# The MLP of a streaming encoder layer: up projection by Strassen's block product, down projection from DRAM, output projection by token halves

## The chip, the cores and the metric

The kernel runs on one core of a Trainium2 chip. The metric is the device time of one execution in microseconds; a kernel's time is the median of its runs. The profile comes from one execution. Its engines are TensorE (PE in the profile, with PEld for its weight loads), VectorE (DVE), ScalarE (ACT), GpSimd (POOL) and SyncE (SP, which here only issues DMAs).

## The reference

One layer of a streaming encoder for two groups, 1024 prompt tokens and 64 sample tokens, all in float32 with a width of 1024:

```python
x = x + mix @ p["w_out"][li]
x = x + cross_attention(rms_norm(x, p["norm_x_g"][li]), mem_k[li], mem_v[li],
                        p["xq_w"][li], p["xo_w"][li])
h = rms_norm(x, p["norm_ffn_g"][li])
x = x + jnp.square(jax.nn.relu(h @ p["w_up"][li])) @ p["w_down"][li]
...
return rms_norm(x, p["final_g"]), ...
```

`mix` comes from three token mixers (a gated recurrence, a convolution, a pooling mixer), which the change doesn't touch. `w_up` is 1024 x 4096, `w_down` 4096 x 1024, and the attention's output weight `xo_w` 1024 x 1024. `rms_norm` multiplies by the reciprocal root of the mean square of a token and by a gain for each channel.

## The kernel before

**Layout.** Activations lie with the channels on the 128 partitions and the 1088 tokens (T) in a row: eight tiles of 128 channels (KT = 8), each in a slot of 1152 floats. The slots are one pool of 35; a tile takes a slot and gives it back after its last reader.

**Products.** Each float32 operand is split in two parts that one pass of TensorE carries: `hi` is a copy on ACT into the type `fp32r`, `lo` the difference on DVE. `mm3` (L186) makes a product from three matmuls: hi by hi, hi by lo, lo by hi. `dense` (L195) makes one output tile of 128 channels: for each of the three token groups of 364, 364 and 360 columns it takes a PSUM bank, adds up 8 x 3 matmuls, and calls an evacuation. With `across` it runs the groups side by side. PSUM has four banks of the tag "d" and four of "m".

**Weights.** `fetch` (L136) loads the next block of 128 x 8 x 128 weights through SP, into one of three buffers; `prep` (L155) makes its hi part on ACT and its lo part on DVE, into one of three buffers each, and fetches the next. `weights` (L168) takes the oldest prepared block. The order of the blocks is `all_weights` (L966).

**Output projection.** `residual` (L741) loads a residual tile, makes one dense output tile, adds the two in the evacuation on DVE, squares the sum on ACT and adds it up on DVE for the norm (`sq_add`), splits it times the gain (`hl`), and stores the tile to DRAM. The norm's root enters later: `rstd_rows` makes one factor for each token, broadcast over the partitions (`rb`).

**MLP.** `mlp` (L886) goes through 8 blocks of 512 hidden channels. For each it makes 4 dense tiles of the up projection; the evacuation multiplies the relu by `rb`, and `squared` squares and splits the result. Then it makes 8 dense tiles of the down projection over these 4 and adds each to the residual in SBUF (`xr`, loaded from DRAM in the first block). The last block goes by other token groups and ends in the final norm and the stores.

**Order.** The scheduler puts each engine's instructions in an order when the program is built, and each engine then runs its own strictly in that order, waiting where a semaphore says so. SP, too, issues its DMAs in order: a DMA that waits holds those behind it.

Of the kernel before, what the change touches and what calls it, by code (L numbers as in the profile page):

```python
# [11 lines left out]
P = 128  # L12
D = 1024
# [22 lines left out]
TT = [(c * P, min(P, T - c * P)) for c in range(9)]  # L36

# [10 lines left out]
class Trunk:  # L48
# [87 lines left out]
    def fetch(self, parts=1):  # L136
        s = next(self.wsrc, None)
# [6 lines left out]
        self.raws.append(raw)  # L144
# [10 lines left out]
    def prep(self, parts=1):  # L155
        if not self.raws:
            return
        raw = self.raws.pop(0)
# [14 lines left out]
    def pump(self):  # L173
        """traces the next steps of each chain that runs beside the dense products"""
# [11 lines left out]
    def mm3(self, out, wh, wl, xh, xl, first, last):  # L186
        mm = self.mm
        mm(out, wh, xh, start=first, stop=False)
        mm(out, wh, xl, start=False, stop=False)
        mm(out, wl, xh, start=False, stop=last)  # L190
# [56 lines left out]
    def sq_add(self, acc, x):  # L247
        """adds x*x to the running sum of squares"""
        if acc is None:
            acc = self.slot(n="acc")  # L250
            self.act(acc[:, :T], x, AF.Square)
            return acc
        sq = self.slot(n="sq")
        self.act(sq[:, :T], x, AF.Square)
        self.tt(acc[:, :T], acc[:, :T], sq[:, :T], ADD)
        return acc

    def hl(self, full, g):
        """parts of full * g that one pass carries exactly"""
# [112 lines left out]
    def sq_two(self, accs, k):  # L372
        """sums of squares in two halves, joined before the last"""
# [41 lines left out]
    def mixers(self, xs):  # L415
# [11 lines left out]
        # convolution inputs  # L427
# [60 lines left out]
    def head(self, h, f, k, q, vT, ons):  # L488
# [18 lines left out]
        # v, token-major  # L507
# [56 lines left out]
        # k, token-major  # L564
# [11 lines left out]
        # states  # L576
# [19 lines left out]
        # outputs, token-major for the norm, then transposed  # L596
# [27 lines left out]
    def conv(self, glus, mix):  # L624
# [12 lines left out]
        # layer norm over the channels, token-major  # L637
# [116 lines left out]
    def attention(self, acc, hs):  # L754
# [19 lines left out]
        # a unit: 4 prompt tiles of one head, or the sample tiles of two heads  # L774
# [20 lines left out]
        return [self.outs[k] for k in range(KT)]  # L795
# [60 lines left out]
    def att_values(self, unit, ph, pl):  # L856
# [5 lines left out]
        for h, s, c, n in jobs:  # L862
            kh, kl = self.kv[g, h]
            for dv in range(2):
                if 2 * h + dv not in self.outs:
                    self.outs[2 * h + dv] = (self.slot(F32R, n="oh"), self.slot(F32R, n="ol"))
                oh, ol = (x[:, s:s + n] for x in self.outs[2 * h + dv])
# [4 lines left out]
                self.act(oh, ps[:, :n], AF.Copy)  # L872
                self.split_lo(ol, ps[:, :n], oh)

# [11 lines left out]
    def mlp(self, acc, hs, x2src):  # L886
        nc = self.nc
        rb = self.rstd_rows([acc], D)
        xr = []
        facc = None  # L890
        for fb in range(NFB):
            ts = []
            for f in range(FB):
                t = self.slot(n="t")

                def ev(b, t0, m):
                    self.stt(t[:, t0:t0 + m], b, 0.0, rb[:, t0:t0 + m], MAX, MUL)
                self.dense(self.weights(), hs, range(KT), ev, across=f == 0 and fb == 0)
                ts.append(self.squared(t, GROUPS if f == FB - 1 else [(0, T)]))
            if fb == 0:  # L900
                for o in range(KT):
                    x = self.slot(n="xr")
                    nc.sync.dma_start(x[:, :T], x2src[o])
# [219 lines left out]
```

## Time and profile before

| | |
|---|---|
| runs, us | 1605.22, 1608.7, 1605.95 (median 1605.95) |
| span of the profiled execution, us | 1606.3 |
| busy, us | PE 1575.2, DVE 781.2, ACT 476.6, POOL 92.0 |
| matmuls | 9732 |
| moved by DMA | 107.47 MB, 67 GB/s over the span |
| square sums of attention's output projection (`acc`), first to last start, us | 738.6 to 823.8 |
| first evacuation of a down product (into `xr`), us | 879.1 |

The profiled execution is known by its span, 1606.3 us; it lies 0.4 us over the median of the runs. A row of a group names line, engine, operation, tiles as out<-in, partitions x elements, and the count; then the busy us in all and the mean ns of one; then the engine's idle us before them, and what ended it. The duration of a matmul covers its whole way through the array, and matmuls overlap: what one costs is the distance from start to start. In a timeline a row begins with its start and its length in us.

### The profile page before, as it was taken

To read this page: it belongs to the slowest core of one execution; us is meant where nothing else is said; L and a number is where in the kernel's file an instruction comes from. 1 tells how busy PE (TensorE), PEld (TensorE's weight loads), DVE (VectorE), ACT (ScalarE), POOL (GpSimd) and SP (SyncE) were. 2 spreads that over 40 slices of the span, in tenths; PEclk is the share of its full clock that TensorE was granted. 3 is DMA by queue.
4 is the path that set the end of the run, shared out by engine and by line. 5 is a ranking of instruction groups with operands and counts; after the bars stand their busy time and mean duration, and the time that the engine had idled before them with its cause. 6 is when DMAs were issued, how large, how long until landed. Compare 5 with 4: busy or idle time off the path is not lost.

```text
span 1606.3 us, 22499 instructions
## 1 busy us (share of the span) xinstructions
PE 1575.2 (98%) x9732; PEld 1542.7 (96%) x9732; DVE 781.2 (49%) x1123; ACT 476.6 (30%) x807; POOL 92.0 (6%) x59
## 2 busy tenths in 40 slices
PE   7899998999999999999999999999999999999997
PEld 7699998899999999989999999999999999999997
DVE  7838868865654433683433333333332433333344
ACT  7611142436262222462232121120301212021144
POOL 2720004100000000000000000000000000000005
PEclk9899999999999999999999999999999999999999
DMA  8421010101013311212424111111111111111103
GB/s 311 144 83 41 28 31 16 41 14 43 29 64 143 123 54 53 79 67 83 152 94 151 40 53 40 40 53 40 41 52 40 45 47 40 53 40 40 53 1 112
DMA packets 37555, 107.47 MB, mean 67 GB/s; under 512 B 5456, under 2 KB 13136, under 8 KB 37456
## 3 DMA queue, kind: packets, MB, share of 16 engines
q1 hardware_dynamic: 34576, 105.38, 19.7%
q8 instruction: 76, 1.25, 0.3%
q10 hardware_dynamic: 2880, 0.66, 0.2%
q14 instruction: 23, 0.19, 0.0%
HBM read 89.94 MB, written 16.08 MB: 66 GB/s over the span
## 4 chain that ended last, share of the span: by engine, by line
PE 85%; issue 9%; DVE 3%; POOL 1%; ACT 1%; DMA 0%; SPq 0%; POOLq 0%; DVEq 0%; ACTq 0%
PE psd L193 75%; PE psm L193 4%; PE psm L530 3%; DVE cacc L130 1%; POOL xr L126 1%; DVE wl L127 1%; PE psm L608 0%; PE psm L610 0%; PE psm L501 0%; PE psd L850 0%; DMA wr<-wk 0%; ACT wh L119 0%; PE psm L619 0%; PE psm L582 0%; PE psm L547 0%
## 5 line engine op out<-in xcount | busy, mean ns | idle before, releaser
L193 PE MATMUL psd<-hi,wl 128*128 128x364 f32 (+3 forms) x2400 | 793.6, 331 | 3.0 <-DVE wl L127 3.0
L193 PE MATMUL psd<-lo,wh 128*128 128x364 f32 (+3 forms) x2400 | 792.9, 330 | 3.3 <-DVE lo L130 3.3
L193 PE MATMUL psd<-hi,wh 128*128 128x364 f32 (+3 forms) x2400 | 793.2, 331 | 0.0
L193 PEld LDWEIGHTS psd<-lo,wh 128*128 128x128 f32 x2400 | 453.1, 189 | 5.0 <-DVE lo L130 4.6
L193 PEld LDWEIGHTS psd<-hi,wl 128*128 128x128 f32 x2400 | 453.6, 189 | 3.6 <-DVE wl L127 3.2
L193 PEld LDWEIGHTS psd<-hi,wh 128*128 128x128 f32 x2400 | 453.7, 189 | 1.2
L119 ACT ACTIVATE wh<-wr 128x1024 fp32r<-128x1024 f32 (+1 forms) x127 | 131.8, 1039 | 815.6 <-PE psd L193 655.5
L127 DVE TENSOR_TENSOR xr<-psd,xr 128x364 f32<-128x364 f32 (+3 forms) x192 | 101.9, 534 | 210.2 <-PE psd L193 210.0
L127 DVE TENSOR_TENSOR wl<-wr,wh 128x1024 fp32r<-128x1024 f32 (+1 forms) x127 | 167.2, 1320 | 66.8 <-ACT wh L119 66.8
L130 DVE SCALAR_TENSOR_TENSOR t<-psd,rb 128x364 f32<-128x364 f32 (+1 forms) x96 | 51.1, 533 | 202.4 <-PE psd L193 202.4
L130 DVE SCALAR_TENSOR_TENSOR cacc<-glu,vecs,cacc 128x1118 f32<-128x1118 f32 x60 | 90.5, 1508 | 0.7
L126 POOL TENSOR_TENSOR xr<-xr,facc 128x416 f32<-128x416 f32 x16 | 19.0, 1224 | 1193.7 <-ACT facc L119 1193.7
L127 DVE TENSOR_TENSOR res<-psd,res 128x364 f32<-128x364 f32 (+1 forms) x45 | 23.2, 533 | 92.2 <-PE psd L193 51.2
L127 DVE TENSOR_TENSOR lo<-t,hi 128x1088 fp32r<-128x1088 f32 (+2 forms) x48 | 43.8, 913 | 39.9 <-ACT hi L119 39.9
L193 PE MATMUL psd<-ol,wh 128*128 128x364 f32 (+1 forms) x168 | 55.2, 329 | 0.0
L193 PE MATMUL psd<-oh,wl 128*128 128x364 f32 (+1 forms) x168 | 55.2, 329 | 0.0
L193 PE MATMUL psd<-oh,wh 128*128 128x364 f32 (+1 forms) x168 | 55.2, 328 | 0.0
L530 PEld LDWEIGHTS psm<-q,fn 128*128 128x128 f32 (+2 forms) x448 | 48.0, 180 | 4.5 <-issue 3.9
L530 PE MATMUL psm<-q,fn 128*128 128x64 f32 (+2 forms) x448 | 49.0, 262 | 2.4 <-DVE tot L127 2.4
L119 ACT ACTIVATE t<-t 128x1088 f32<-128x1088 f32 (+2 forms) x48 | 38.3, 799 | 35.1 <-DVE t L130 35.1
L130 DVE SCALAR_TENSOR_TENSOR qf<-psd,rb 128x364 f32<-128x364 f32 (+1 forms) x24 | 12.7, 535 | 57.1 <-PE psd L193 57.1
L119 ACT ACTIVATE hi<-t 128x1088 fp32r<-128x1088 f32 (+2 forms) x48 | 38.9, 810 | 1.5
(214 smaller groups left out, 1442.7 us busy)
## 6 DMA issues: line engine op xcount, KB each, us to landing
wr<-w_up SPq DMA_DIRECT2D x32, 512.0 KB, 3.6
wr<-w_down SPq DMA_DIRECT2D x32, 512.0 KB, 3.5
wr<-w_in SPq DMA_DIRECT2D x22, 512.0 KB, 3.5
x<-res SPq DMA_DIRECT2D x16, 544.0 KB, 2.7
x<-xT SPq DMA_DIRECT2D x8, 544.0 KB, 7.3
res<-xT SPq DMA_DIRECT2D x8, 544.0 KB, 5.1
res<-x SPq DMA_DIRECT2D x8, 544.0 KB, 4.9
xr<-x SPq DMA_DIRECT2D x8, 544.0 KB, 7.6
```

Of the source, the lines that this page charges most:

```text
L119: return self.inorder("act", lambda: self.nc.scalar.activation(out, in_, f, **kw))
L126: return self.inorder("pool", lambda: eng.tensor_tensor(out, a, b, op))
L127: return self.inorder("dve", lambda: self.nc.vector.tensor_tensor(out, a, b, op))
L130: return self.inorder("dve", lambda: self.nc.vector.scalar_tensor_tensor(out, in0, s, in1, op0, op1))
L193: return self.inorder("pe", lambda: self.nc.tensor.matmul(*args, **kw))
L530: mm(pv[:m, c], k[:, c * P:c * P + m], qc[:, :, 1, :], start=True, stop=True)
```

## The change

The change has three parts.

1. **Output projection by halves.** The 1088 tokens are two halves of 544 (H), each of two quarters of 272 (Q). `project` makes the output projection for one half, in groups of 272 columns, with two output tiles in one slot; the weights `xo` are therefore fetched and prepared twice. `attention` writes its results into tiles by half, so the unit of tokens 512 to 1023 is evacuated in pieces of 32 and 480 columns.
2. **Up projection by Strassen's product** (Winograd's form). `normed_half` now multiplies the norm into the activations. `operands` takes the 2 x 2 blocks of a half (channels 0 to 511 and 512 to 1023 by quarter) and makes the seven right operands from them: four differences (two on DVE, two on POOL), then hi on ACT and lo on DVE of all seven, 14 slots for a half. `pair_units` takes the weights of a pair of output tiles as 2 x 2 blocks, makes four sums on POOL and splits seven left operands in four units "12", "56", "73" and "4". `up` runs seven products of 12 matmuls with 272 columns for each pair and half, in the order 1, 5, 6, 2, 7, 3, 4. Several products add up in one bank (A: 1, 6, 7, 4; C: 5, 3; B: 2), and the partial sums are evacuated in between, on ACT or DVE. The last steps form relu(v) times v on DVE, and each half of a pair is stored to DRAM (`tdram`, "tt" in the rows). The first two pairs run for half 0 alone at the start and for half 1 alone at the end; 14 pairs run for both.
3. **Down projection as a stage of its own.** `mlp` calls `up`, then loads the residual and, block by block, the four tiles of t, splits them and makes the down products as before. Block 0 goes last.

```diff
+H = T // 2
+Q = H // 2
+NPAIR = 16
+LATE = 2
+FBS = list(range(1, NFB)) + [0]
...
+    def project(self, c, os, src, spill):
...
+            self.dense(self.weights(), os, range(KT), ev, groups=[(0, Q), (Q, Q)])
+            acc = self.sq_add(acc, x, H)
+            if o % 2:
+                nc.sync.dma_start(spill[o - 1:o + 1, :, cols].rearrange("o p t -> p o t"), xs[-1])
...
+    def normed_half(self, acc, xs, g):
+        r = self.rstd_cols([acc], CT, D, "m")
...
+        for k in range(KT):
+            x = xs[k // 2][:, k % 2]
+            self.stt(x, x, self.vec(g, k), rb[:, :H], MUL, MUL)
...
+    def operands(self, xs):
...
+        b11, b12, b21, b22 = block(0, 0), block(0, 1), block(1, 0), block(1, 1)
+        r = {}
+        r["1"] = split(b11)
+        t1, w1 = diff(b12, b11)
+        r["5"] = split(t1, w1)
+        t3, w3 = diff(b22, b12, gp)
+        t2, w2 = diff(b22, t1)
+        r["6"] = split(t2, w2)
+        r["2"] = split(b21)
+        t4, w4 = diff(b21, t2, gp)
+        r["7"] = split(t3, w3)
+        r["3"] = split(b22)
+        r["4"] = split(t4, w4)
...
+    def pair_units(self):
...
+        self.tt(s12[:, :4], rj[:, :4], rj[:, 4:], ADD, gp)
+        self.tt(s12[:, 4:], s12[:, :4], ri[:, :4], SUB, gp)
+        self.tt(s34[:, :4], ri[:, :4], rj[:, :4], SUB, gp)
+        self.tt(s34[:, 4:], ri[:, 4:], s12[:, 4:], SUB, gp)
...
+        for src, k0, names in ((ri, 0, "12"), (s12, 0, "56"), (s34, 0, "73"), (rj, 4, "4")):
...
+            self.act(hi[:, :n], src[:, k0:k0 + n], AF.Copy)
+            self.split_lo(lo[:, :n], src[:, k0:k0 + n], hi[:, :n])
...
+    ORDER = "1562734"
+    BANK = {"1": "A", "5": "C", "6": "A", "2": "B", "7": "A", "3": "C", "4": "A"}
...
+    def up(self, xs, tdram):
+        jobs = [(p, (0,)) for p in range(LATE)] + [(p, (0, 1)) for p in range(LATE, NPAIR)]
+        jobs += [(p, (1,)) for p in range(LATE)]
...
+            for i, m in enumerate(self.ORDER):
+                for c in cs:
...
+                    for k in range(4):
+                        self.mm3(banks[b][:, :Q], wh[:, k], wl[:, k], th[:, k], tl[:, k], k == 0 and m in "152", k == 3,
...
+                    if m in "1564":
+                        self.act({"1": c11, "5": c22, "6": c12, "4": c21}[m], ps, AF.Copy)
+                    else:
+                        d = {"2": c11, "7": c22, "3": c12}[m]
+                        self.tt(d, ps, d, ADD)
+                    if m in "34":
+                        v = t[:, "34".index(m)]
+                        self.stt(v, v, 0.0, v, MAX, MUL)
...
+            for c in cs:
+                self.nc.sync.dma_start(tdram[2 * p:2 * p + 2, :, c * H:c * H + H].rearrange("o p t -> p o t"), st[c][1])
...
+        nxt = block(FBS[0])
+        for i, fb in enumerate(FBS):
+            ts = nxt
+            if i < NFB - 1:
+                nxt = block(FBS[i + 1])
...
+        for c in range(2):
+            acc, xs = self.project(c, o[c], x1, x2)
...
+            if c == 0:
+                halves[0] = operands()
+        self.mlp(halves, x2)
```

**What moves, at three places.** The first is DVE in the output projection. Before, each tile's three evacuations (`res<-psd,res`) are followed by a weight split, the square sum and one low part, and then by the next tile's evacuations:

```order
L127 TENSOR_TENSOR res_6304<-psd_6364,res_6304 128x360
L127 TENSOR_TENSOR wl_6401<-wr_5323,wh_6400 128x1024
L127 TENSOR_TENSOR acc_6297<-acc_6297,sq_6390 128x1088
L130 SCALAR_TENSOR_TENSOR lo_6394<-res_6304,vecs,hi_6393 128x1088
L127 TENSOR_TENSOR res_6398<-psd_6406,res_6398 128x364
L127 TENSOR_TENSOR res_6398<-psd_6432,res_6398 128x364
L127 TENSOR_TENSOR res_6398<-psd_6458,res_6398 128x360
```

In the changed kernel, DVE at the start of half 1: `df` is a difference of operands(), `tl` a low part of one of the seven operands of half 0, and `res_6802` the first output tiles of half 1.

```order
L133 TENSOR_TENSOR tl_6765<-df_6761,th_6764 128x1088
L133 TENSOR_TENSOR df_6771<-res_6476,df_6761 128x544
L133 TENSOR_TENSOR df_6771<-res_6601,df_6761 128x544
L133 TENSOR_TENSOR tl_6775<-df_6771,th_6774 128x1088
L133 TENSOR_TENSOR tl_6779<-res_6476,th_6778 128x544
L133 TENSOR_TENSOR tl_6779<-res_6601,th_6778 128x544
L133 TENSOR_TENSOR tl_6788<-df_6768,th_6787 128x1088
L133 TENSOR_TENSOR tl_6792<-res_6476,th_6791 128x544
L133 TENSOR_TENSOR tl_6792<-res_6601,th_6791 128x544
L133 TENSOR_TENSOR tl_6798<-df_6784,th_6797 128x1088
L133 TENSOR_TENSOR res_6802<-psd_6810,res_6802 128x272
L133 TENSOR_TENSOR res_6802<-psd_6836,res_6802 128x272
```

All of half 0's normalising steps, differences and low parts stand ahead of the first evacuation of half 1.

The second place is DVE at the start of the up stage. Before, it holds each up tile's three evacuations (`t<-psd,rb`), one weight split and one low part:

```order
L130 SCALAR_TENSOR_TENSOR t_7083<-psd_7090,rb_6977 128x364
L130 SCALAR_TENSOR_TENSOR t_7083<-psd_7116,rb_6977 128x364
L130 SCALAR_TENSOR_TENSOR t_7083<-psd_7142,rb_6977 128x360
L127 TENSOR_TENSOR wl_7175<-wr_6874,wh_7174 128x1024
L127 TENSOR_TENSOR lo_7169<-t_7083,hi_7168 128x1088
```

In the changed kernel, DVE behind the second pair (`t_7428`) and ahead of the third: the eight normalising steps of half 1 (`res` by `rb_7563`) and its first operands.

```order
L136 SCALAR_TENSOR_TENSOR t_7428<-t_7428 128x544
L136 SCALAR_TENSOR_TENSOR res_6802<-res_6802,vecs,rb_7563 128x544 x2
L136 SCALAR_TENSOR_TENSOR res_6926<-res_6926,vecs,rb_7563 128x544 x2
L136 SCALAR_TENSOR_TENSOR res_7051<-res_7051,vecs,rb_7563 128x544 x2
L136 SCALAR_TENSOR_TENSOR res_7176<-res_7176,vecs,rb_7563 128x544 x2
L133 TENSOR_TENSOR tl_7582<-res_6802,th_7581 128x544
L133 TENSOR_TENSOR tl_7582<-res_6926,th_7581 128x544
L133 TENSOR_TENSOR df_7587<-res_6802 128x544
L133 TENSOR_TENSOR df_7587<-res_6926 128x544
L133 TENSOR_TENSOR tl_7591<-df_7587,th_7590 128x1088
```

Half 1 is normalised only after both single-half pairs, and its operands come in one piece behind that.

The third place is SP at the first down product. Before, the residual loads stand between weight loads, and the down product's other operand never leaves SBUF:

```order
L153 DMA wr_7268<-w_up 128x1024
L903 DMA xr_7359<-x_3903 128x1088
L903 DMA xr_7361<-x_3903 128x1088
L903 DMA xr_7363<-x_3903 128x1088
L903 DMA xr_7365<-x_3903 128x1088
```

In the changed kernel, SP from the last store of t (`tt<-t_10859`) on; `t_11003` to `t_11009` are the four tiles of the first block of the down stage.

```order
L1048 DMA tt<-t_10859 128x2x544
L1065 DMA xr_10981<-x_3903 128x1088
L1065 DMA xr_10983<-x_3903 128x1088
L159 DMA wr_10989<-w_down 128x1024
L159 DMA wr_10995<-w_down 128x1024
L159 DMA wr_11001<-w_down 128x1024
L1060 DMA t_11003<-tt 128x1088
L1060 DMA t_11005<-tt 128x1088
L1060 DMA t_11007<-tt 128x1088
L1060 DMA t_11009<-tt 128x1088
```

The loads that the first down product needs stand behind the last store of the up stage and five other loads.

More of the change, by code (lines that the diff above doesn't have):

```diff
@@ L36 @@
 TT = [(c * P, min(P, T - c * P)) for c in range(9)]
+H = T // 2
+Q = H // 2
+CT = [(c * P, min(P, H - c * P)) for c in range(5)]
+NPAIR = 16
+LATE = 2
+FBS = list(range(1, NFB)) + [0]
 VEC = {}
@@ L136, in fetch @@
     def fetch(self, parts=1):
-        s = next(self.wsrc, None)
+        kind, s = next(self.wsrc, (None, None))
         if s is None:
@@ L794, in attention @@
         self.seq = None
-        return [self.outs[k] for k in range(KT)]
+        return [[self.out(c, k) for k in range(KT)] for c in range(2)]
     def load_kv(self, group, h):
@@ L871, in att_values, with two, out @@
                              ph[:, mt * 512 + c:mt * 512 + c + n], pl[:, mt * 512 + c:mt * 512 + c + n], mt == 0, mt == 1)
-                self.act(oh, ps[:, :n], AF.Copy)
-                self.split_lo(ol, ps[:, :n], oh)
+                for k in range(2):
+                    a, b = max(s, k * H), min(s + n, k * H + H)
+                    if a < b:
+                        oh, ol = (x[:, a - k * H:b - k * H] for x in self.out(k, 2 * h + dv))
+                        self.act(oh, ps[:, a - s:b - s], AF.Copy)
+                        self.split_lo(ol, ps[:, a - s:b - s], oh)
+    def two(self, dt=F32, n="s"):
+        return self.slot(dt, n=n)[:, :2 * H].rearrange("p (k t) -> p k t", k=2)
+    def out(self, c, k):
+        if (c, k // 2) not in self.outs:
+            self.outs[c, k // 2] = (self.two(F32R, "oh"), self.two(F32R, "ol"))
+        return [x[:, k % 2] for x in self.outs[c, k // 2]]
     def squared(self, t, cuts):
@@ new lines, in operands, with block, four, parts @@
+    def operands(self, xs):
+        gp = self.nc.gpsimd
+        def block(kh, n):
+            return [xs[2 * kh + j][:, :, n * Q:n * Q + Q] for j in range(2)]
+        def four(dt, n):
+            return self.slot(dt, n=n)[:, :4 * Q].rearrange("p (k t) -> p k t", k=4)
+        def parts(t):
+            return [t[:, 0:2], t[:, 2:4]]
+        def diff(a, b, eng=None):
+            t = four(F32, "df")
+            for d, x, y in zip(parts(t), a, b):
+                self.tt(d, x, y, SUB, eng)
+            return parts(t), t
+        def split(ps, whole=None):
+            hi, lo = four(F32R, "th"), four(F32R, "tl")
+            if whole is not None:
+                self.act(hi, whole, AF.Copy)
+                self.split_lo(lo, whole, hi)
+            else:
+                for h, l, x in zip(parts(hi), parts(lo), ps):
+                    self.act(h, x, AF.Copy)
+                    self.split_lo(l, x, h)
+            return hi, lo
+        b11, b12, b21, b22 = block(0, 0), block(0, 1), block(1, 0), block(1, 1)
[11 more added lines that the diff above has]
+        r["4"] = split(t4, w4)
+        return r
@@ L889, in mlp, with block @@
+    def mlp(self, xs, x2src):
+        nc = self.nc
+        tdram = self.dp.tile([4 * NFB, P, T], F32, name="tt")
+        self.up(xs, tdram)
         xr = []
-        facc = None
-        for fb in range(NFB):
+        def block(fb):
             ts = []
@@ L894, in mlp @@
                 t = self.slot(n="t")
[L896 to L903, printed above, removed]
-                    xr.append(x)
-            if fb < NFB - 1:
+                nc.sync.dma_start(t[:, :T], tdram[FB * fb + f])
+                ts.append(t)
+            return [self.hl(t[:, :T], None) for t in ts]
+        for o in range(KT):
+            x = self.slot(n="xr")
+            nc.sync.dma_start(x[:, :T], x2src[o])
+            xr.append(x)
+        for _ in range(3):
+            self.prep()
+        nxt = block(FBS[0])
[3 more added lines that the diff above has]
+                nxt = block(FBS[i + 1])
                 for o in range(KT):
```

118 lines of the change are left out of this document (87 added, 31 removed).

## The prediction

> **What bounds the kernel now.** I read the head of the page first, then the busy times by stretch.
>
> ```profile
> span 1606.3 us, 22499 instructions
> PE 1575.2 (98%) x9732; PEld 1542.7 (96%) x9732; DVE 781.2 (49%) x1123; ACT 476.6 (30%) x807; POOL 92.0 (6%) x59
> PE 85%; issue 9%; DVE 3%; POOL 1%; ACT 1%; DMA 0%; SPq 0%; POOLq 0%; DVEq 0%; ACTq 0%
> ```
>
> TensorE is busy for 98% of the span and holds 85% of the chain that ends last. What a change is worth here is what it does to the time in which TensorE issues matmuls. In the MLP there is no hole at all:
>
> ```profile
> 900.00:1000.00 100.00, 100.00 (x604) 100.00 (x603) 35.30 (x54) 17.76 (x20) 0.00 (x0) 1.00 0.15 48
> 1000.00:1100.00 100.00, 100.00 (x604) 100.00 (x603) 35.16 (x53) 17.76 (x20) 0.00 (x0) 1.00 0.14 43
> ```
>
> The columns are us, then busy us and count of PE, PEld, DVE, ACT and POOL, then granted clock, DMA share and GB/s. 604 matmuls in 100 us are 0.1656 us each, at full clock, for 364, 364 and 360 columns in turn (363 on the mean). DVE works 35 us of 100 and POOL not at all, so a steady stage has room for Strassen's additions. The price of other widths is read from the starts in the timeline:
>
> ```profile
> 701.50 0.28 PE L193 MATMUL psm<-kvh,lo 128*128 128x256 f32 x1
> ...
> 702.93 0.28 PE L193 MATMUL psm<-kvh,lo 128*128 128x256 f32 x1
> 1560.30 0.35 PE L193 MATMUL psd<-hi,wfh 128*128 128x416 f32 x1
> ...
> 1562.18 0.35 PE L193 MATMUL psd<-lo,wh 128*128 128x416 f32 x1
> ```
>
> Twelve steps of 256 columns take 1.43 us, 0.119 each; ten of 416 take 1.88 us, 0.188 each. So a matmul costs what its columns cost, about 0.43 ns apiece, and some 10 ns more. For 272 columns I take 0.126 us (0.119 and 16 columns).
>
> **The products.** The up projection goes from 32 x 3 x 24 = 2304 matmuls (381.5 us) to 16 pairs x 2 halves x 7 products x 12 = 2688 of 272 columns (338.7 us): 42.8 us less, not the eighth (47.7) of the plain count. The output projection keeps its columns but goes from 576 matmuls (95.4 us) to 768 (96.8 us): 1.4 us more. Together 41.4 us are gained, if nothing else ends later. Against this speaks the Trainium skill, "TensorE: Matmul & The Clock Gate", section "Back-to-back issue gap": a sustained stream of weight loads and matmuls is said to go at 81 ns for 128 columns and 131 for 512. Read between those (an estimate from the page), 363 columns cost 112 ns and 272 cost 100, and the two projections would lose 23 us. The 0.188 us at 416 columns contradicts it here, and the rows decide.
>
> **The prices of the other work.** Additions, splits and evacuations go by these rows; shapes between them are scaled by their elements:
>
> ```profile
> L127 DVE TENSOR_TENSOR kvl<-kv,kvh 128x1024 fp32r<-128x1024 f32 x8 | 9.6, 1218 | 4.5 <-ACT kvh L119 4.4
> L127 DVE TENSOR_TENSOR lo<-t,hi 128x1088 fp32r<-128x1088 f32 x24 | 31.0, 1292 | 22.1 <-ACT hi L119 22.1
> L127 DVE TENSOR_TENSOR tot<-fs 128x544 f32<-128x544 f32 x4 | 2.8, 712 | 0.0
> L130 DVE SCALAR_TENSOR_TENSOR lo<-res,vecs,hi 128x1088 fp32r<-128x1088 f32 x16 | 21.5, 1345 | 1.7 <-ACT hi L119 1.7
> L127 DVE TENSOR_TENSOR xr<-psd,xr 128x256 f32<-128x256 f32 x8 | 3.3, 419 | 1.8 <-PE psd L193 1.8
> L127 DVE TENSOR_TENSOR xr<-psd,xr 128x364 f32<-128x364 f32 x112 | 59.6, 535 | 127.8 <-PE psd L193 127.8
> L130 DVE SCALAR_TENSOR_TENSOR t<-psd,rb 128x364 f32<-128x364 f32 x64 | 34.1, 534 | 109.4 <-PE psd L193 109.4
> L119 ACT ACTIVATE wh<-wr 128x1024 fp32r<-128x1024 f32 x121 | 128.3, 1060 | 814.7 <-PE psd L193 655.5 <-issue 144.8 <-PE psm L193 9.8
> L119 ACT ACTIVATE hi<-t 128x1088 fp32r<-128x1088 f32 x24 | 26.7, 1113 | 0.8
> L119 ACT ACTIVATE wh<-wr 128x512 fp32r<-128x512 f32 x6 | 3.5, 620 | 0.8 <-DMA wr<-wk 0.8
> L119 ACT ACT_TABLE_LOAD x24 | 30.8, 1283 | 1.1 <-PEq L1113 0.7
> L126 POOL TENSOR_TENSOR xr<-xr,facc 128x416 f32<-128x416 f32 x16 | 19.0, 1224 | 1193.7 <-ACT facc L119 1193.7
> ```
>
> **What goes and what is hidden.** The 96 relu evacuations with the norm (0.53 us each) and the squares go; TensorE waits for none of them in the stretches above, so that is worth 0. The down stage now loads and splits t: for each block 4 x 1.3 on DVE, beside 4 weight splits (4.9) and 24 additions (12.8), 23 us under 288 matmuls (47.7 us). It stays hidden, also its 2.2 MB of loads a block, except for the first block (border 3).
>
> **The steady pairs.** A steady pair of both halves holds 168 matmuls, 21.2 us. In it DVE splits 3.5 weight parts (4.3 us), adds 6 products out of PSUM (0.43 each, 2.6) and does 4 relu-squares of 544 (0.7 each, 2.8): 9.7 us. ACT has 3.7 us of weight copies and 8 evacuations of about 0.4; POOL 4 differences of 512 (about 1.3 each by the 416-wide row). All three fit into 21.2. The tightest place is the second half's seventh product: it waits for the sixth's evacuation, which stands on ACT behind the split of unit "4" (0.62), and that waits for the second product. It has 1.5 us for about 1.3, so I price the 13 steady pairs (3 to 15) at 0 (0 to 4 in all). The borders don't fit.
>
> *Border 1, the second half of the output projection.* On DVE the whole of operands() for half 0 stands ahead of the first evacuation of half 1. It is 8 normalising steps (0.7 each: 5.6), 10 steps of 544 (7.1), 4 of 1088 (5.2) and 2 weight splits (2.4): 20.3 us. It can begin only after the square sum, the table load (1.28), two reciprocals, the broadcast and its copy, about 7 us into half 1. So the first bank comes free at about 7 + 20.3 + 0.4 = 28 us. TensorE has four banks there: 4 x 24 x 0.126 = 12.1 us of work and 0.6 for the norm, then it waits. That is 15 us. POOL's four differences can add to it:
>
> ```profile
> 51.46 24.56 POOL L126 TENSOR_TENSOR x<-x,rb 128x1088 f32<-128x1088 f32 x7 [14.21 <-ACT rb L119]
> 53.88 9.28 DVE L127 TENSOR_TENSOR wl<-wr,wh 128x1024 fp32r<-128x1024 f32 x3 [1.17 <-ACT wh L119]
> 66.63 3.50 DVE L127 TENSOR_TENSOR wl<-wr,wh 128x1024 fp32r<-128x1024 f32 x1
> 66.00:79.00 13.00, 6.70 (x21) 5.35 (x20) 13.00 (x6) 10.96 (x13) 13.00 (x5) 0.62 0.18 48
> ```
>
> Beside POOL a split of 1024 lasts 3.5 us in place of 1.2, about as long as POOL's own operation: two such steps of SBUF inputs take turns. Four differences of 544 at about 1.35 are up to 5 us more. I take 18 (13 to 21).
>
> What one engine hands to the next costs some 0.2 us: in the timeline the bank's last matmul is followed by the next bank's at 761.60, and DVE starts on the full bank at 761.80.
>
> ```profile
> 761.60 0.33 PE L193 MATMUL psd<-oh,wh 128*128 128x364 f32 x1
> 761.80 0.53 DVE L127 TENSOR_TENSOR res<-psd,res 128x360 f32<-128x360 f32 x1 [3.25 <-PE psd L193]
> ```
>
> *Border 2, the first three pairs.* In a single-half pair (84 matmuls, 10.6 us) the seventh product follows the second directly, so the ACT order just named costs 0.2 + 0.62 + 0.4 = 1.2 us a pair. In pair 0 the split of unit "56" also stands on ACT behind the first product's evacuation (0.2 + 0.4 + 1.06: 1.7), and DVE is pressed: 5 us for pairs 0 and 1. In pair 2 half 1's operands are needed, and DVE makes them only now: after the broadcast 1 us of copies, 5.6 of normalising, 1.4 for the first low part (product 1 at 8 us); a difference, an ACT copy and a low part (1.4 + 1.1 + 1.3: product 5 at 12); then a difference, a waiting split and a low part more (product 2 at 17); and the evacuations before product 6 stand on ACT behind the last split, which waits for POOL (21). TensorE has six products of 1.5 us in that time, 9 us. That is 12 us, with POOL's turns up to 17; I take 14. Together 19 (12 to 24). The last two single pairs cost 1.2 each: 2.5 (1 to 4).
>
> *Border 3, from up to down.* The first down product needs a block of t out of DRAM. On SP its four loads stand behind the last store, and that waits for the last relu-square. This one follows the last ACT copy and a weight split on DVE (0.2 + 0.4, then 1.2 begun before it, then 0.7), so it ends about 1.8 us after the last matmul. Between the store and the first load stand two xr and three weights. What a queue of such loads takes:
>
> ```profile
> L903 SPq DMA_DIRECT2D xr<-x x8: 382/440/737, 864.8 to 868.4; - x8
> DMA to landing us min/median/max: 4.5/7.6/10.5
> 870.00:875.00 5.00, 5.00 (x32) 5.00 (x32) 1.61 (x3) 2.00 (x4) 0.00 (x0) 1.00 1.01 409
> ```
>
> Eight loads of 557 KB land over 10.5 us after issue, at up to 409 GB/s. Store, two xr, three weights and the first t are 3.8 MB, 9.3 us; with 1.8, issue and landing about 14 us. Then ACT's copy (1.1); the other three t follow at 1.4 us each, with copy and low part (1.1 + 1.3) behind the last. TensorE could have done its first 31 matmuls (5.1 us) by then: 14 + 4.2 + 2.4 - 5.1 = 15.5. I take 16 (11 to 19); below, if the two xr and the weights overtake the store.
>
> *The clock.* In the window quoted above, with TensorE idle half of the time, the granted clock is 0.62. Three long waits should each leave some 3 us at half speed: 5 us (0 to 8). What attention's evacuations gain in number (32 columns here, 480 there) lies on ACT and DVE, which are not full there: 0.
>
> **The sum.** -42.8 + 1.4 + 18 + 19 + 2.5 + 16 + 5 = +19.1 on the profiled execution's 1606.3: 1625.4. The median of the runs is 1605.95, 0.4 under it: 1625. The lower ends give -41.4 + 37 = -4, 1602; the upper ones -41.4 + 80 = +39, 1645.
>
> **The rivals.**
> Faster: DVE's backlog at borders 1 and 2 is covered after all. What speaks for it is that DVE is busy for only 49% of the span; against it, that the splits stand in one queue ahead of what TensorE waits for. If both borders cost nothing the sum is -41.4 + 2.5 + 16 + 2 = -21: 1585. It decides from where the two together cost less than about 20 us, in place of 37. Chance 0.16.
> The reload is not late, because the loads of t reach the queue ahead of the store: 16 and a third of the clock's 5 are gone, 1607 to 1608. Against it stands the order of SP, for it only that many slots are free by then. Chance 0.12.
> Each steady pair waits too, since one late evacuation on ACT holds the seventh product: 1.2 us in 13 pairs, +16, 1641; with POOL's turns on DVE twice that. Against it the 0.2 us of slack. Chance 0.08.
> A matmul has a fixed price, so that 272 columns cost what 363 do: (2688 + 768) x 0.04 = +137 on the sum, 1762. The widths 256, 363 and 416 above say no: 0.01. The page of the Trainium skill named above leans this way; by its rates the sum would come to about 1690.
> That the change does not do what it says has no room: the rows of the new order show the seven products.
>
> **How the numbers follow.** The forecast has 0.63. Faster by over 0.2% (about what a measurement of this kernel can tell from no change, 3.2 us) takes the first rival and a sliver of the second: 0.17. Within 0.2%: 0.06, from the second. Slower: 0.77. The range 1597 to 1648 leaves out most of the first rival (0.12) and the far end of the third and the fourth (0.06). The forecast's own range is 1610 to 1645.
>
> **What would show it.** In the profile after: matmuls of 272 columns 0.126 us apart and 21.2 us a steady pair; a hole of 15 to 20 us on TensorE some 12 us into half 1 of the output projection, ended by DVE's evacuation; a stuttering stretch before the third pair; a hole of about 16 us before the first down product, ended by the low part of t; a granted clock under 1 behind each. No such holes, or a spacing over 0.13, would make it wrong.

## The result and the profile after

| | before | changed |
|---|---|---|
| median of the runs, us | 1606.63 | 1626.38 (1624.51 to 1629.08) |
| ratio, with its 95% interval | | 1.0118 (1.0102 to 1.0135) |
| span of the profiled execution, us | 1606.3 | 1627.2 |

The change costs 20 us; the prediction had 1625. The runs of one kernel can lie in two groups with different mean granted clocks, about 5 us apart in experiment 8 (1590 and 1595) and 8 us in experiment 11 (1581 twice, 1589 three times), so a difference of that size is read from the traces as well. The head of the page of the changed kernel:

```profile
span 1627.2 us, 24362 instructions
PE 1550.3 (95%) x10312; PEld 1513.6 (93%) x10312; DVE 918.6 (56%) x1280; ACT 533.9 (33%) x951; POOL 230.2 (14%) x139
```

TensorE has 25 us less to do (1575.2 before), and the span is 21 us longer. The steady part of the up stage, and four places that are not steady, in the columns of the windows shown of before:

```profile
960.00:1060.00 100.00, 100.00 (x796) 100.00 (x795) 50.48 (x66) 30.64 (x55) 30.68 (x18) 1.00 0.29 106
876.00:915.00 39.00, 29.20 (x179) 27.01 (x178) 33.54 (x37) 14.61 (x24) 17.35 (x9) 0.78 0.16 55
724.00:731.00 7.00, 7.00 (x31) 6.53 (x31) 2.07 (x6) 2.09 (x6) 0.00 (x0) 0.51 0.00 0
799.00:814.00 15.00, 0.12 (x1) 0.15 (x1) 13.82 (x16) 6.40 (x8) 2.67 (x2) 0.51 0.32 108
1221.00:1229.00 8.00, 0.47 (x1) 0.47 (x2) 0.49 (x1) 1.38 (x2) 0.00 (x0) 0.50 1.02 415
```

The first row has no hole and full clock; the other four are the third pair (876 to 915), the end of the attention, the start of the output projection's second half, and the step from up to down. In each of these four the mean clock is well under 1. What TensorE waited for, in the view of waits (us in all, times, longest):

```profile
PE psd L199 <- DVE res L133: 17.5, 1, 17.5
PE psd L199 <- ACT hi L125: 16.3, 1, 16.3
PE psm L199 <- DVE tl L133: 7.7, 4, 3.1
PE psd L199 <- ACT t L125: 1.8, 1, 1.8
```

These are the three borders. In the timeline, DVE at the first and the second, and SP, ACT and TensorE at the third:

```profile
789.61 6.77 DVE L136 SCALAR_TENSOR_TENSOR res<-res,vecs,rb 128x544 f32<-128x544 f32 x8 [3.23 <-ACT rb L125]
796.30 2.49 DVE L133 TENSOR_TENSOR tl<-res,th 128x544 fp32r<-128x544 f32 x2
...
813.31 1.47 DVE L133 TENSOR_TENSOR res<-psd,res 128x272 f32<-128x272 f32 x4
...
878.63 0.72 DVE L136 SCALAR_TENSOR_TENSOR t<-t 128x544 f32<-128x544 f32 x1
879.27 5.65 DVE L136 SCALAR_TENSOR_TENSOR res<-res,vecs,rb 128x544 f32<-128x544 f32 x8
...
903.56 2.36 DVE L133 TENSOR_TENSOR tl<-df,th 128x1088 fp32r<-128x1088 f32 x1
...
1215.11 0.37 SPq L1048 DMA_DIRECT2D tt<-t  x1
1215.57 1.30 SPq L1065 DMA_DIRECT2D xr<-x  x2
1216.92 1.73 SPq L159 DMA_DIRECT2D wr<-w_down  x3
1218.75 11.64 SPq L1060 DMA_DIRECT2D t<-tt  x11
1227.37 1.11 ACT L125 ACTIVATE hi<-t 128x1088 fp32r<-128x1088 f32 x1 [13.90 <-DMA t<-tt]
1228.53 1.58 PE L199 MATMUL psd<-hi,wh 128*128 128x364 f32 x4 [16.32 <-ACT hi L125]
```

From 789.6 to 813.3 DVE does nothing but half 0's operands and two weight splits, 23.7 us, and then empties four full banks in a row. From 879.3 to 905.9 it makes half 1's operands, with one weight split between them, 26.6 us. In the last six rows the third border is seen on SP, ACT and TensorE: the loads of t are issued 3.6 us after the last store, and the first lands 8.6 us later.

### The profile page after: what moved, and what is told of

It is laid out like the page before. It is cut to its first block, busy times and chain, and to the rows that moved or that the text cites. A ratio compares the mean times of both kernels' runs of the same rounds, so it can differ in the third digit from the quotient of the medians.

```text
span 1627.2 us, 24362 instructions
## 1 busy us (share of the span) xinstructions
PE 1550.3 (95%) x10312; PEld 1513.6 (93%) x10312; DVE 918.6 (56%) x1280; ACT 533.9 (33%) x951; POOL 230.2 (14%) x139
## 3 DMA queue, kind: packets, MB, share of 16 engines
q1 hardware_dynamic: 51664, 147.32, 25.9%
## 4 chain that ended last, share of the span: by engine, by line
PE 84%; DVE 6%; issue 6%; DMA 1%; POOL 1%; ACT 1%; SPq 0%; POOLq 0%; DVEq 0%; ACTq 0%
PE psd L199 64%; PE psm L199 13%; PE psm L536 3%; DVE wl L133 1%; DVE tl L133 1%; POOL xr L132 1%; DVE cacc L136 1%; DMA wr<-wk 1%; PE psm L614 1%; DMA t<-tt 1%; PE psm L616 0%; DVE res L136 0%; PE psm L507 0%; PE psm L625 0%; PE psd L856 0%
## 5 line engine op out<-in xcount | busy, mean ns | idle before, releaser
L199 PE MATMUL psd<-hi,wh 128*128 128x364 f32 (+2 forms) x1632 | 541.2, 333 | 16.3 <-ACT hi L125 16.3
L199 PE MATMUL psd<-lo,wh 128*128 128x364 f32 (+2 forms) x1632 | 541.2, 332 | 4.2 <-DVE lo L136 4.2
L199 PE MATMUL psd<-hi,wl 128*128 128x364 f32 (+2 forms) x1632 | 541.9, 332 | 3.0 <-DVE wl L133 3.0
L199 PEld LDWEIGHTS psd<-hi,wh 128*128 128x128 f32 x1632 | 310.0, 190 | 17.6 <-ACT hi L125 16.5
L199 PEld LDWEIGHTS psd<-lo,wh 128*128 128x128 f32 x1632 | 309.5, 190 | 6.1 <-DVE lo L136 5.5
L199 PEld LDWEIGHTS psd<-hi,wl 128*128 128x128 f32 x1632 | 309.8, 190 | 3.6 <-DVE wl L133 3.2
L199 PE MATMUL psm<-tl,wh 128*128 128x272 f32 x448 | 131.1, 293 | 7.7 <-DVE tl L133 7.7
L199 PE MATMUL psd<-th,wh 128*128 128x272 f32 x448 | 130.8, 292 | 1.8 <-ACT t L125 1.8
L199 PE MATMUL psm<-th,wh 128*128 128x272 f32 x448 | 131.6, 294 | 0.3 <-ACT th L125 0.2
L199 PE MATMUL psm<-th,wl 128*128 128x272 f32 x448 | 131.0, 292 | 0.0
L199 PE MATMUL psd<-oh,wh 128*128 128x272 f32 x256 | 75.1, 294 | 17.5 <-DVE res L133 17.5
```

The costliest lines, as they stand in the source:

```text
L199: return self.inorder("pe", lambda: self.nc.tensor.matmul(*args, **kw))
```

## The experiments

All differences are against the changed kernel's 1626.4 us unless another kernel is named.

### 1. The reload earlier

```diff
 def up(...):
+            if n == NPAIR:                       # first of the two last half-1 pairs
+                pre = self.block(tdram, FBS[0])  # the four loads of t
 def mlp(...):
-        nxt = block(FBS[0])
+        nxt = [self.hl(t[:, :T], None) for t in pre]
```

> The four loads of t for the first block of the down stage are put ahead of the two last half-1 pairs, so that they no longer stand behind the last store and the residual loads. My theory (border 3: the hole of 16.5 us is the way of t through the queue): the hole shrinks to what ACT's copy (1.1 us) and DVE's low part (1.3) need behind the last evacuation, 3 to 5 us; with a clock that no longer drops (about 1.5) the kernel takes 12 to 15 us less, 1611 to 1614. Rival (the DMA engines are the bound: eight residuals, three weight blocks and t are 8 MB in any order, 20 us at the 409 GB/s seen): the hole moves to the first evacuation, which waits for the residual, or to the weights of the last pairs, and less than 5 us are gained, 1621 or more.

Measured: 1612.5 us, 13.9 less. What TensorE still waits for at that place:

```profile
PE psd L203 <- ACT hi L129: 2.3, 1, 2.3
PE psd L203 <- DVE lo L137: 0.9, 1, 0.9
```

The copy behind the last evacuation and its low part are left, as expected, and the residuals and weights, now loaded behind t, are not late. What is late now is the second block of t, which still stands behind them on SP: ACT waits for it, and one new wait of TensorE follows, 1.1 us for an evacuation into `xr`. So the hole was the place of t in the queue, not the amount of data.

### 2. Half 0's operands between the tiles

```diff
-            if c == 0:
-                halves[0] = operands()
+            halves.append(operands())        # now a generator of 14 portions
 def project(...):
             acc = self.sq_add(acc, x, H)
+            if c == 1:
+                next(halves[0], None)
+                next(halves[0], None)
```

> The operands of half 0 are made in sixteen portions, two behind each output tile of half 1's output projection, in place of one lump ahead of it. My theory (border 1: DVE's lump of 24 us stands ahead of the first evacuation): a tile takes TensorE 6.05 us and DVE 2.8, so a portion of 2.6 fits beside each; the hole of 17.6 us goes and the 2.9 us of low clock behind it: 19 to 21 us less, 1605 to 1608. Rival (the work is on the path either way, DVE has no room beside POOL's turns): eight waits of 1 to 2 us appear, or the first pair of the up stage waits for operands that are late; 5 to 10 us less, 1616 to 1621.

Measured: 1611.0 us, 15.4 less. The wait for `res` is gone; in the view of windows the stretch of the old hole is full (TensorE busy for 40.00 of 40.00 us):

```profile
780.00:820.00 40.00, 40.00 (x320) 39.81 (x320) 32.49 (x43) 17.79 (x24) 9.49 (x6) 1.00 0.46 153
```

In the view of waits one row is new:

```profile
PE psm L203 <- DVE acc L137: 3.4, 1, 3.4
```

DVE does the same work beside TensorE's. The portions behind the last tiles delay half 1's square sum, and the norm's first matmul waits 3.4 us for it. That wait and the half clock behind it (3.41 us, from 832.1) are most of what is missing from the expected 19 to 21.

### 3. Half 1's operands in portions, over seven pairs

```diff
-LATE = 2
+LATE = 7
-FBS = list(range(1, NFB)) + [0]
+FBS = list(range(4, NFB)) + list(range(4))
 def up(...):
+                if n < LATE and m in "14":
+                    next(halves[1], None)
```

> Half 1's operands are made in portions of two per pair during seven single-half pairs (in place of a lump behind two), and the same seven pairs run for half 1 alone at the end. My theory (border 2 is DVE's lump): a single-half pair has 10.6 us on TensorE and 7 on DVE, and a portion is 2.9; the stalls of 13.6 us and some 4 of low clock go, the two at pair 0 stay: 14 to 17 us less, 1609 to 1612. Rival (a single-half pair is already full, since ACT's order or POOL's turns on DVE cost 1.2 us in each): fourteen single pairs at 1.2 us are +17 and eat the gain, 1622 to 1630.

Measured: 1637.2 us, 10.9 more. My theory fell: the lump is gone, but the pairs got longer. From the first product of the up stage to the first one that reads half 1's operands lie 103.6 us, where seven single-half pairs and the one product of 12 matmuls ahead of it need 75.7 at 0.126 us a matmul.

```profile
L203 PE MATMUL psd<-th,wh x448: 283/289/596, 851.5 to 1142.4; 128*128 128x272 f32 x150
L203 PE MATMUL psm<-th,wh x448: 286/289/394, 955.1 to 1222.0; 128*128 128x272 f32 x150
```

(The last two times of a row are the first and the last start.) The timeline of DVE and POOL in one of the last pairs, where no portion is made, shows what fills a pair:

```profile
1179.42 1.82 DVE L140 SCALAR_TENSOR_TENSOR t<-t 128x544 f32<-128x544 f32 x1
...
1184.27 1.28 POOL L136 TENSOR_TENSOR sw<-wr,sw 128x512 f32<-128x512 f32 x1
1184.29 2.33 DVE L137 TENSOR_TENSOR wl<-wr,wh 128x1024 fp32r<-128x1024 f32 x1 [0.53 <-ACT wh L129]
1186.55 0.78 DVE L137 TENSOR_TENSOR t<-psm,t 128x272 f32<-128x272 f32 x2
1188.00 1.22 DVE L137 TENSOR_TENSOR wl<-sw,wh 128x1024 fp32r<-128x1024 f32 x1
1191.00 1.82 DVE L140 SCALAR_TENSOR_TENSOR t<-t 128x544 f32<-128x544 f32 x1
```

The split that stands ahead of the evacuation takes 2.33 us beside POOL's 1.28 and 1.22 when POOL is idle. So the evacuation of product 7 (`t<-psm,t` at 1186.55) comes late, the pair's last product, 4, which adds up in the same bank, starts 0.9 us late, and the pair takes 11.58 us (1179.42 to 1191.00) in place of 10.6. Four of the seven last pairs lose this much; the other three lose nothing. The Trainium skill, "SBUF — State Buffer", section "SBUF: two separate sides", has a rule for it: a DVE instruction with two SBUF inputs and a GpSimd instruction that reads SBUF lock each other out, and whichever starts first has the shared ports for its whole length. The split of 2.33 us, begun 0.02 us after POOL's instruction of 1.28, against 1.22 alone agrees with it.

### 4. All three

The edits of 1, 2 and 3 in one kernel:

```diff
-LATE = 2
+LATE = 7
 def up(...):
+            if n == NPAIR:
+                pre = self.block(tdram, FBS[0])
...
+                if n < LATE and m in "14":
+                    next(halves[1], None)
 def project(...):
+            if c == 1:
+                next(halves[0], None)
+                next(halves[0], None)
```

> The three edits together. My theory (three borders that add up): the gains add, 45 to 53 us less than the changed kernel, 1573 to 1581, which is some 2% under the kernel before. Rival (DVE's work is only pushed on, each border hands its backlog to the next): the sum falls short by 10 us or more, 1591 or higher.

Measured: 1611.1 us, 15.2 less and 30 short of the expectation. The third edit's loss takes back about half of what the other two gain (29.3 us); in the up stage TensorE waits 17.3 us for DVE's and ACT's evacuations into `t` in these two rows, as in experiment 3:

```profile
PE psd L203 <- DVE t L137: 11.3, 6, 2.3
PE psd L203 <- ACT t L129: 6.0, 2, 3.7
```

### 5. Eight banks

```diff
 def dense(...):
-                b = self.bank("d")
+                b = self.bank("m" if tag == "dm" and t0 else "d")
 def project(...):
-            self.dense(self.weights(), os, range(KT), ev, groups=[(0, Q), (Q, Q)])
+            self.dense(self.weights(), os, range(KT), ev, groups=[(0, Q), (Q, Q)], tag="dm" if c else "d")
```

> The second half of the output projection takes its two banks per tile from both tags, one from each, so that eight banks stand in place of four; DVE's order stays. My theory of border 1 (hole = DVE's lump less what the free banks let TensorE do): four banks more are 12.1 us more of matmuls, the hole shrinks from 17.6 us to about 5.5, and the kernel takes 11 to 15 us less, 1611 to 1615. Rival (DVE's work itself is on the path, whatever TensorE does meanwhile): TensorE gets ahead, but waits as long later, for the evacuations or for the sum of the norm, and less than 4 us are gained, 1622 or more.

Measured: 1616.7 us, 9.7 less. In the view of waits `res` stands at 7.6 us in place of 17.5:

```profile
PE psd L207 <- DVE res L141: 7.6, 1, 7.6
```

Its timeline of DVE, from the first normalising step to the first evacuation:

```profile
784.28 6.77 DVE L144 SCALAR_TENSOR_TENSOR res<-res,vecs,rb 128x544 f32<-128x544 f32 x8 [3.23 <-ACT rb L133]
...
809.04 1.21 DVE L141 TENSOR_TENSOR wl<-wr,wh 128x1024 fp32r<-128x1024 f32 x1
810.17 0.43 DVE L141 TENSOR_TENSOR res<-psd,res 128x272 f32<-128x272 f32 x1
```

Four banks took off 9.9 of the 12.1 us. The rest is DVE's lump, which now lasts 25.9 us (784.28 to 810.17): since TensorE gets two tiles further, two more weight splits of 1.2 us stand in it. This shows border 1 as the difference of a lump on DVE and the cover that the banks give, without a change in the work.

### 6. The differences on DVE

```diff
 def operands(...):
-        gp = self.nc.gpsimd
+        gp = None          # DVE
```

> The differences that operands() gives to POOL go to DVE, four instructions of 544 for each half, about 0.67 us each; nothing else moves. As the prediction had it (POOL's turns are up to 5 us of border 1, of which I took 3): DVE's lump loses the turns and gains 2.7 us, so the two borders stay within 3 us of what they are, 1622 to 1628. Rival (turns cost more than the work is worth): low parts go back from 2.4 us to 1.3 at both borders, and 4 to 8 us go, 1618 or less. Second rival (POOL's help is a real relief): 3 to 6 us more, 1629 or more.

Measured: 1627.5 us, the same. In DVE's timeline the lump goes from 23.7 to 22.8 us:

```profile
787.54 5.66 DVE L144 SCALAR_TENSOR_TENSOR res<-res,vecs,rb 128x544 f32<-128x544 f32 x8 [3.22 <-ACT rb L133]
793.12 1.35 DVE L141 TENSOR_TENSOR tl<-res,th 128x544 fp32r<-128x544 f32 x2
...
810.36 1.48 DVE L141 TENSOR_TENSOR res<-psd,res 128x272 f32<-128x272 f32 x4
```

The first two low parts last 1.35 us in place of 2.49, the eight normalising steps 5.66 in place of 6.77, and four differences of 0.67 are added. POOL's help and its turns come out even here, within 1 us.

### 7. Seven pairs without POOL

```diff
 def pair_units(...):          # and operands(), as in 6
-        gp = self.nc.gpsimd
+        gp = None
```

This stands on the kernel of experiment 3.

> The kernel with seven single-half pairs and half 1's operands in portions (1637 us), but with the weight sums and the differences on DVE in place of POOL. Theory now (POOL's turns stretch DVE's splits in a single-half pair from 1.2 to 2.3 us, so that the pair has no room): the four waits of 1.0 us in the last pairs go, the first seven pairs, 95 us in that kernel, come down to 80 to 85; 1620 to 1626. Rival (it is DVE's own load and the place of the portion ahead of an evacuation): DVE now has 13 us of work in a single-half pair of 10.6, the first seven pairs take 95 us or more as before, 1633 or more.

Measured: 1615.2 us, 22 less than experiment 3 and 11.2 less than the changed kernel; the gain is larger than I had expected. The up stage's first products, as shown of experiment 3, and DVE's timeline in one of the last pairs:

```profile
L207 PE MATMUL psd<-th,wh x448: 282/289/394, 844.5 to 1117.4; 128*128 128x272 f32 x150
L207 PE MATMUL psm<-th,wh x448: 286/289/292, 928.8 to 1193.0; 128*128 128x272 f32 x150
```

```profile
1150.21 0.72 DVE L144 SCALAR_TENSOR_TENSOR t<-t 128x544 f32<-128x544 f32 x1
1154.00 0.69 DVE L141 TENSOR_TENSOR sw<-wr 128x512 f32<-128x512 f32 x1
1158.27 1.23 DVE L141 TENSOR_TENSOR wl<-wr,wh 128x1024 fp32r<-128x1024 f32 x1 [0.52 <-ACT wh L133]
1160.81 0.73 DVE L144 SCALAR_TENSOR_TENSOR t<-t 128x544 f32<-128x544 f32 x1
```

The first stretch takes 84.3 us in place of 103.6, and a last pair 10.60 (1150.21 to 1160.81) in place of 11.58. A sum of 512 costs DVE 0.69 us and POOL 1.28 or more, and while POOL does it DVE's splits wait. In these pairs the work on POOL was no relief. In the last pairs POOL had only the weight sums; for the first seven, sums and differences were moved together, and what each was worth there was not separated. ACT's order was the same in both kernels, and a last pair without POOL has no wait, so ACT's order does not hold a product there.

### 8. Two borders mended

The edits of 1 and 2, with the first block's copies and low parts in the last pair and half 0's portions ended before the last tile:

```diff
 def project(...):
+            for _ in range((1, 2, 2, 3, 2, 2, 2, 0)[o] if c == 1 else 0):
+                next(halves[0], None)
 def up(...):
+            if n == NPAIR:
+                pre = self.block(tdram, FBS[0])
...
+                if n == len(jobs) - 1 and m in "1562":
+                    pre.append(self.hl(pre.pop(0)[:, :T], None))
```

> The changed kernel with the early loads of t, whose copies and low parts now go into the last half-1 pair, and with half 0's operands in portions that end before the last tile of the output projection. My theory: the gains of the two single edits add (13.9 and 15.4 us), and the hole of 3.7 us at the norm's sum and 2 to 3 of the 4.9 us left at the first down product go too: 1588 to 1594, 0.7 to 1.2% less than the kernel before. Rival (the early copies and low parts make the last pair late, the portions crowd each other): 1597 or more.

Measured: 1594.9 us, ratio to before 0.9908 (0.9891 to 0.9925). The hole at the first down product is gone, but the wait for the square sum stays (3.2 us), so ending the portions one tile earlier did not free DVE in time. The median lies 1 us above the expected 1588 to 1594.

### 9. An eighth product

```diff
-                    for k in range(4):
+                    for k in list(range(4)) * (2 if m == "2" else 1):
```

> The changed kernel with the second product of every pair and half computed twice over into the same bank (the first pass is overwritten): eight products of 12 matmuls in place of seven, the plain count of multiplications, everything else alike. My theory (TensorE is the bound in the 14 double pairs, and a matmul of 272 columns costs 0.126 us): 384 matmuls more are 48.4 us; the first three pairs, which wait anyway, hide 2 to 5 of them; 1669 to 1675. Rival (the steady pairs have waits that a shorter stream only uncovers, so that the seventh of the work is not worth its count): under 40 us more, 1666 or less.

Measured: 1670.5 us, 44.1 more. In the traces the up stage is 45.1 us longer, so 3.3 of the 48.4 us are hidden in the first three pairs, as expected. The evacuations of the same product in two successive pairs, first of the changed kernel, then with the eighth product:

```profile
935.32 0.40 ACT L125 ACTIVATE t<-psd 128x272 f32<-128x272 f32 x1 [0.53 <-PE psd L199]
...
956.50 0.40 ACT L125 ACTIVATE t<-psd 128x272 f32<-128x272 f32 x1 [0.53 <-PE psd L199]
```

```profile
982.39 0.40 ACT L134 ACTIVATE t<-psd 128x272 f32<-128x272 f32 x1 [0.53 <-PE psd L208]
...
1006.61 0.40 ACT L134 ACTIVATE t<-psd 128x272 f32<-128x272 f32 x1 [0.53 <-PE psd L208]
```

A double pair takes 21.18 us with seven products and 24.22 with eight: 3.04 us for 24 matmuls, 0.127 each. In the steady pairs Strassen's product is worth its full count.

### 10. Three borders, all on DVE

The edits of 7 and 8 together:

```diff
-LATE = 2
+LATE = 7
 def pair_units(...):          # and operands()
-        gp = self.nc.gpsimd
+        gp = None
 def project(...):
+            for _ in range((1, 2, 2, 3, 2, 2, 2, 0)[o] if c == 1 else 0):
+                next(halves[0], None)
 def up(...):
+            if n == NPAIR:
+                pre = self.block(tdram, FBS[0])
...
+                if n < LATE and m in "14":
+                    next(halves[1], None)
...
+                if n == len(jobs) - 1 and m in "1562":
+                    pre.append(self.hl(pre.pop(0)[:, :T], None))
```

> The early reload, half 0's portions between the tiles, seven single-half pairs with half 1's portions, and all weight sums and differences on DVE, POOL out of it. My theory (three separate borders, and POOL's turns as what spoiled the third edit): against the kernel of seven pairs without POOL (1615.2) the 17 us of the first hole with 2 to 3 of clock and the 16.5 of the last with 1.5 go, less 3 to 4 that stay at the norm's sum: 1580 to 1586, about 1.5% less than the kernel before. Rival (DVE is now full in the second half of the output projection, 22 us for the tiles and 23 for the portions in 48 us, and the early low parts and single pairs press on it too): 1590 or more, no better than the kernel with two borders mended.

Measured: 1581.3 us, 45 less than the changed kernel; ratio to before 0.9835 (0.9821 to 0.9848). The head of its page, and TensorE's longest wait from the output projection's second half on:

```profile
span 1580.2 us, 24375 instructions
PE 1542.7 (98%) x10312; PEld 1506.6 (95%) x10312; DVE 962.7 (61%) x1400; ACT 550.7 (35%) x971; POOL 91.5 (6%) x59
```

```profile
PE psm L208 <- DVE acc L142: 2.7, 1, 2.7
```

TensorE does the same 10312 matmuls as in the changed kernel. DVE has 44 us more work and POOL 139 us less, and what is left of the borders as waits is one of 2.7 us and some of under 1. The first seven pairs still take 87.8 us for matmuls that cost 74.1; 9.0 of the difference lie in the first pair, where half 1's norm, that wait and the low clock behind it stand.

### 11. Portions spilled into the first pair

On the kernel of experiment 10:

```diff
 def project(...):
-            for _ in range((1, 2, 2, 3, 2, 2, 2, 0)[o] if c == 1 else 0):
+            for _ in range((1, 2, 2, 2, 2, 1, 0, 0)[o] if c == 1 else 0):
 def up(...):
+                    while m not in ready[c]:
+                        next(halves[c])
```

> As the kernel with everything on DVE, but fewer portions lie between the tiles and none behind the last two; the operands still missing are made in the first pair, each ahead of the product that reads it. My theory (the wait of 3.4 us at the norm's sum comes from portions behind the last tiles): that wait goes down to 1 us, the first pair waits 1 to 2 us more for its late operands, in all 0 to 3 us less than the kernel with everything on DVE. Rival (the first pair is the tighter place): 2 us more or worse.

Measured: 1589.1 us, 7.7 more by the median. The wait for the sum falls from 2.7 us to 0.8, so the portions behind the last tiles were what delayed it, but the first pair now waits for a weight split that stands behind the late operands:

```profile
PE psd L208 <- DVE wl L142: 4.1, 4, 3.1
```

The traces of experiments 10 and 11, laid side by side, lie 6.9 us apart. The seven first pairs take 93.7 us in place of 87.8 (2.5 of it in the first pair), and the attention's end 1.6 more, at half clock for 10.2 us in place of 6.8, which the edit doesn't touch. So in these traces the rival is right, and the pairs are the tighter place. The runs at 1581 are no slower than experiment 10 and left no trace, so why they are faster stays open.

## Why the prediction was right, step by step

| term | predicted, us | measured, us | from |
|---|---|---|---|
| up products | -42.8 | -44.2 | 383.1 before (0.1663 a matmul), 338.9 after (0.1261) |
| output projection's products | +1.4 | +1.1 | 768 x 0.1261 for 576 x 0.1663 |
| border 1 | +18 | +17.6 | gap on TensorE, 796.14 to 813.88 |
| border 2, and the last two single pairs | +21.5 | +13.6 | gaps from 853 to 905; none in the last two |
| border 3 | +16 | +16.5 | gap 1211.93 to 1228.53 |
| clock behind the borders | +5 | +9.3 | 2.9 and 2.1 from the half clock behind borders 1 and 3; 4.3 at border 2, what is left of 20.2 us lost up to 915 after the gaps and the norm's 20 small matmuls (2.2) |
| attention's end | 0 | about +4.6 | 67.3 us from the first score product to the first output product; before, 65.8 to the attention's last product, with 19 output products (3.2) among its own; 3.4 is lost to half clock |
| ahead of the attention | 0 | +2.8 | first score product at 665.9 and 663.1 |

The measured terms come to 21.3, and the norm's small matmuls, 40 in place of 36, add 0.4; the spans differ by 20.9.

**The products.** The price by columns held. I had read 0.1656 for the wide matmul from a window's count, which includes those that reach over its edges; 4320 of them from the first up product to the last block, with the norm's 36 small ones taken off, give 0.1663. Experiment 9 shows that the seven eighths are worth 44 us as long as TensorE is the bound, so the rival of a fixed price is out.

**Border 1** was right in mechanism and size, and experiments 2 and 5 show both halves of it: DVE's lump, and the cover of four banks. POOL's turns, which I took as 3 us on top, were 1.1 on the normalising steps and 1.1 to 1.2 on a low part beside POOL, but experiment 6 shows that without POOL the same time goes into its work.

**Border 2** was right in place and chain (third pair, waits for low parts `tl`), and mis-sized: 13.6 us and 4.3 of clock, against 21.5 with the last two pairs. The third pair's own gaps, 13.0 us, are near the 14 that I took. The step that failed is the price of a single-half pair, "1.2 us a pair" from ACT's order. The last two took 10.6 us each without a wait, and the first two together lost 1.4 us beside the norm's small matmuls, not 5. ACT in the last pair, with the split of unit "4" and the evacuation of product 6:

```profile
1206.08 0.63 ACT L125 ACTIVATE wh<-wr 128x512 fp32r<-128x512 f32 x1 [0.99 <-PE psm L199]
1206.62 0.38 ACT L125 ACTIVATE t<-psm 128x272 f32<-128x272 f32 x1
```

I had the split wait for product 2, whose last matmul starts at 1207.39. It starts 0.2 us after the last matmul of product 6 (1205.88), so the evacuation ends at 1207.00, 0.5 us before product 7 starts (1207.52).

Where single pairs follow each other for longer (experiment 3) four of the last seven do lose 1.0 us each, but the cause is POOL's turn on DVE's split, as experiment 7 shows by taking POOL away. Experiment 3 fell for that reason: I had added up DVE's 7 us and a portion of 2.9 against 10.6 and left out that POOL's 6 to 7 us lie in the same pair.

**Border 3** was right in cause and size: experiment 1 takes 13.9 us away by the place in the queue alone. Inside the sum the first copy of t starts 15.4 us after the last product, not 14, and TensorE doesn't wait again behind it, where I had 1.5 us for the other copies and the low part; the hole is ended by ACT's copy, not by the low part.

**The clock** was another miss: 9.3 us behind the borders where I had 5, since border 2 is not one wait but several, with the clock at half in between. These 4.3 and the 4.6 at the attention's end, put at 0, made up for the 7.9 that border 2 fell short of. The 2.8 ahead of the attention lie in code that the change doesn't touch. That the total was right within 2 us is in part this luck.

**The rivals.** "Faster" asked that borders 1 and 2 be covered; they weren't. Experiments 2, 3 and 7 show what covering takes: portions in place of lumps for both, and for border 2 also more pairs and POOL out of the way. The reload was late, as SP's order had it. The steady pairs had no wait, as forecast, with 21.18 us each.

## What to carry to other kernels

A faster product pays its full count where TensorE is the bound, and the cost lies at the stage borders: look there for one engine's lump of work ahead of what TensorE waits for, and cut the lump into portions that fit beside each tile (15 us here for one, and 45 with all three borders). Before filling an engine's free time, add to its busy time that of the engine that takes turns with it (here POOL with DVE); moving small sums and differences from POOL back to DVE made the same order of portions 22 us faster. A result that goes through DRAM should be loaded back ahead of the loads that nobody waits for yet (14 us here).

## What the runs showed of the hardware

- The granted clock falls to half for stretches of 3.41 us or multiples of it (3.41, 6.83, 10.24, 13.65, 17.07, 20.48 in these traces). In waits of TensorE of 7.6 us and more it falls 2 to 5 us into the wait, and the first 3 to 6 us of matmuls behind the wait run at half speed. The Trainium skill, "TensorE: Matmul & The Clock Gate", section "What's actually happening", gives a free-running window of 3413 ns; the lengths agree. But at the attention's end the clock fell in 9 of 13 traces, with no wait of TensorE over 0.5 us ahead of it in the changed kernel's (724 to 731 us, from 690 on); why these and not the others is left open.
- The same unchanged first part of the program, up to the first score product, took from 658.5 us (experiment 8) to 665.9 (changed kernel). A difference of a few us between two spans says nothing until the parts are laid side by side.
- A sum or difference of 512 elements takes 1.28 us or more on POOL (experiment 3) and 0.69 on DVE (experiment 7); beside POOL's, a DVE split of 1024 goes from 1.22 to 2.33.
